# A transformer block on one Trainium2 core: branch projections in a written order, and the first group of gate reordered

## The chip, the core and the metric

The kernel is one program on one core of a Trainium2 chip. The core has five engines with instruction queues of their own: TensorE (PE) multiplies matrices, VectorE (DVE), ScalarE (ACT) and GpSimd (POOL) work on tiles elementwise, and SyncE (SP) issues the DMA transfers between the chip's memory (DRAM) and the on-chip buffer SBUF. Matrix products arrive in PSUM, eight banks of 128 x 512 floats. Each queue runs strictly in its own order; an instruction whose operand is not there holds up all behind it. The metric is the device time of one launch in microseconds (us), less is better.

## The reference

One layer of a diffusion backbone in fp32: 1024 latent tokens of width 1024 and 256 context tokens. After a modulated norm and one input projection come two branches, a neighbourhood attention (`o_na`) and a gated linear attention (`o_gla`). The part that matters here follows:

```python
y = sigmoid(m_a) * (o_na @ w_br_na) + sigmoid(m_b) * (o_gla @ w_br_gla)   # 512 -> 1024, twice
x = x + g1 * (y @ w_o)                                                    # 1024 -> 1024
h2 = modulate(rmsnorm(x, norm2_g), sh2, sc2)
x = x + g2 * ((silu(h2 @ w_gate) * (h2 @ w_up)) @ w_down)                 # 1024 -> 2816 -> 1024
```

## The kernel before

**Products in three passes.** Each fp32 operand is split into a high part (an ACT cast) and a low part (what is left, `raw - hi`, mostly on DVE, in places on POOL). A product is the sum of three matmul passes: high x high, high x low and low x high (`mm3`). So a weight page costs a DMA to one of three raw buffers (`load_raw`, 512 KB), a cast and a subtraction before PE can use it.

**Branch stage** (`branch_units`, before lines 1017 to 1048). For each branch b, half c of the output features, half hf of the tokens and block m, one tile of 128 features x 512 tokens: 12 matmuls into a bank of the pool `mm` (two banks, `psb`), then the merge: y = (1 + ta) * psb for the first branch, and for the second ta = (1 + ta) * psb and y = y + ta. `ta` is a gate tile that earlier code left in DRAM (`ma_d`, `mb_d`). That makes 32 tiles. The second weight half of a branch is split into the buffers of the first (`bufs=4`: two pages, high and low), so the splits can start only when the first half is used up. The output weights `w_out` are loaded after that, scaled by g1 on POOL (L1169), cast and subtracted, 8 pages. Nothing of this stage is written in an order across engines: a scheduler places the instructions by its own estimates of time.

**Output projection and norm** (`project`, `features2`): `pso` is y times the scaled output weights; its result goes to `h2`, the operand of the feed-forward part.

**First group of gate and up.** The feed-forward products use a Strassen-like scheme: for a group of 256 columns of `w_gate` or `w_up`, seven products P1 to P7 of 512-wide blocks take the place of eight. The right operands are B11, B21, B22 and the differences T1 to T4 of `h2`; the left operands are sums of weight blocks (`sums`, tiles `sc` on DVE), split into pages `w_P` (`put`). The results are added up through banks X, Y, Z and W:

```python
X = P1 + P2;  u2 = P1 + P6 (bank Y);  u3 = u2 + P7 (bank Z) + P5 (bank W)
u6 = u2 + P4 (bank Z again);  u2 = u2 + P3 (bank W again)
```

So P4 may write Z only after DVE has added P7's Z, and P3 may write W only after P5's W. P1 and P2 of groups 0 and 1 are made ahead. In this stretch PE, DVE and ACT are `in_order`: the program's order is their order. For group 0 the low parts of gate are on DVE and ACT in the written list (`parted`), those of up on POOL; the DVE list ends after gate's group 0, and the scheduler places later DVE work, the sums of group 1 among it, anywhere after the last operand split (`marks["split"]`).

**Down projection** (`multiply`): seven passes over 11 groups; the lower weight rows of each group are loaded to tiles of their own (`wr`).

## Time and profile before

| | us |
|---|---|
| median of 3 runs | 1617.56 (1615.93 to 1619.08) |
| the profiled execution | 1613.99 |
| its span, first to last instruction | 1612.2 |
| PE busy | 1534.8 (95%) |
| DVE busy | 1012.3 (63%) |
| ACT busy | 638.4 (40%) |
| POOL busy | 518.2 (32%) |

A trace row names the line, the engine, the operation and output<-inputs by the names in the program; L136 is the helper through which PE, DVE and ACT issue, so rows are told apart by tile names. `psd` is the input projection of the gates, `psb` the branch stage, `pso` the output projection, `fX` to `fW` gate and up, `psdn` the down projection. In brackets stands how long the engine was idle before the row and what ended it. Matmuls overlap: one takes 0.39 us, and the next starts 0.23 us later.

### The profile page before, as it was taken

The page shows a single profiled execution, that of the slowest core. Times are in us where ns is not written, and L with a number is a line of the kernel's source. Part 1 is how long each engine was busy: PE and PEld are TensorE (multiplying, and loading weights), DVE is VectorE, ACT ScalarE, POOL GpSimd, SP SyncE. Part 2 cuts the span into 40 slices and gives each one's busy share as a digit, 9 for nine tenths or more (in the row PEclk, how much of TensorE's full clock was granted, in tenths as well). Part 3 has the DMA queues.
Part 4 walks back from the last instruction along what each step waited for, and adds up shares of the span by engine and source line. Part 5 has one row for each costly group of instructions (what it writes and reads, how often), then busy time and mean ns, then how long its engine had stood idle before and what let it go on. Part 6 is the DMA issues. An engine that isn't in the chain of part 4 may idle for free. (4 is left out here: it accounts for less than half of the span.)

```text
span 1612.2 us, 21617 instructions
## 1 busy us (share of the span) xinstructions
PE 1534.8 (95%) x7884; PEld 1253.3 (78%) x7884; DVE 1012.3 (63%) x1593; ACT 638.4 (40%) x1221; POOL 518.2 (32%) x345
## 2 busy tenths in 40 slices
PE   6998999999989998999989997899999999999998
PEld 3777777888878786878868885788888888887886
DVE  4755567238877755453475677766666665778356
ACT  3433453148777752132122334233333323344442
POOL 3333000022111211210041423455555555255444
PEclk9999999999999999999999998999999999999999
DMA  9456576454333336516542333323333333774342
GB/s 332 129 174 209 183 244 216 137 155 126 108 113 104 96 101 202 164 60 215 190 163 80 117 121 113 124 97 109 106 120 108 98 98 118 249 273 150 96 147 98
DMA packets 171667, 235.49 MB, mean 146 GB/s; under 512 B 15580, under 2 KB 105628, under 8 KB 171560
## 3 DMA queue, kind: packets, MB, share of 16 engines
q1 hardware_dynamic: 171560, 234.11, 44.8%
q8 instruction: 62, 1.02, 0.3%
q14 instruction: 45, 0.37, 0.1%
HBM read 167.83 MB, written 66.24 MB: 145 GB/s over the span
## 5 line engine op out<-in xcount | busy, mean ns | idle before, releaser
L136 PE MATMUL psdn<-wd,a 128*128 128x512 f32 x924 | 211.7, 390 | 3.5 <-DVE a L136 1.5
L136 PEld LDWEIGHTS psdn<-wd,a 128*128 128x128 f32 x924 | 172.9, 188 | 42.2 <-DVE a L136 3.2
L210 POOL TENSOR_TENSOR w_P<-sc,w_P 128x512 fp32r<-128x512 f32 x84 | 122.4, 1459 | 131.0 <-ACT w_P L136 131.0
L136 PE MATMUL fZ<-T,w_P 128*128 128x512 f32 x528 | 129.9, 396 | 17.0 <-DVE u L136 17.0
L136 PE MATMUL psd<-hh,w_hi 128*128 128x512 f32 x320 | 132.8, 415 | 0.0
L136 PEld LDWEIGHTS fZ<-T,w_P 128*128 128x128 f32 x528 | 100.4, 191 | 39.9 <-issue 12.1
L210 POOL TENSOR_TENSOR w_lo<-raw,w_hi 128x1024 fp32r<-128x1024 f32 x24 | 57.7, 2408 | 219.0 <-ACT w_hi L136 206.9
L136 PE MATMUL psd<-hh,w_lo 128*128 128x512 f32 x320 | 127.5, 398 | 0.0
L136 PE MATMUL psj<-w_hi,hh 128*128 128x512 f32 x320 | 126.5, 397 | 0.6 <-ACT hh L136 0.6
L136 PE MATMUL psd<-hl,w_hi 128*128 128x512 f32 x320 | 126.6, 396 | 0.0
L136 PE MATMUL psj<-w_lo,hh 128*128 128x512 f32 x320 | 126.1, 394 | 0.3 <-POOL w_lo L210 0.3
L136 PE MATMUL psj<-w_hi,hl 128*128 128x512 f32 x320 | 125.7, 396 | 0.6 <-DVE r L136 0.3
L210 POOL TENSOR_TENSOR w_P<-raw,w_P 128x512 fp32r<-128x512 f32 x57 | 87.9, 1542 | 76.5 <-ACT w_P L136 75.2
L136 ACT CAST w_P<-sc 128x512 fp32r<-128x512 f32 x88 | 54.5, 621 | 139.1 <-PE fZ L136 80.6
L136 DVE TENSOR_TENSOR a<-ar,a 128x512 fp32r<-128x512 f32 x77 | 66.4, 870 | 59.6 <-ACT a L136 59.5
L136 PE MATMUL fX<-B,w_P 128*128 128x512 f32 x432 | 103.8, 389 | 0.0
L248 POOL TENSOR_TENSOR r<-r,nhalf 128x8 f32<-128x8 f32 (+1 forms) x40 | 50.6, 1268 | 150.3 <-DVE r L136 150.3
L136 PEld LDWEIGHTS fX<-B,w_P 128*128 128x128 f32 x432 | 81.1, 188 | 16.8
L136 ACT CAST a<-ar 128x512 fp32r<-128x512 f32 x77 | 47.9, 622 | 112.9 <-PE psdn L136 64.5
L136 ACT CAST w_hi<-raw 128x1024 fp32r<-128x1024 f32 x56 | 58.3, 1050 | 56.0 <-DMA raw<-in_w_in_dram 16.2
L210 POOL TENSOR_TENSOR wd<-wr,wd 128x512 fp32r<-128x512 f32 x39 | 59.3, 1526 | 50.7 <-ACT wd L136 50.4
L136 DVE SCALAR_TENSOR_TENSOR t1f<-t1f,u 128x512 f32<-128x512 f32 x66 | 59.6, 903 | 21.3 <-ACT t1f L136 20.3
(262 smaller groups left out, 3472.3 us busy)
## 6 DMA issues: line engine op xcount, KB each, us to landing
wm<-in_w_mod_dram SPq DMA_DIRECT2D x48, 512.0 KB
raw<-in_w_in_dram SPq DMA_DIRECT2D x40, 512.0 KB
ar<-s_d SPq DMA_DIRECT2D x77, 256.0 KB
raw<-in_w_gate_dram SPq DMA_DIRECT2D x22, 512.0 KB
raw<-in_w_up_dram SPq DMA_DIRECT2D x22, 512.0 KB
s_d<-t1f SPq DMA_DIRECT2D x44, 256.0 KB
s_d<-sa SPq DMA_DIRECT2D x33, 256.0 KB
xt<-in_x_dram SPq DMA_DIRECT2D x16, 512.0 KB
```

The source lines that it names most:

```text
L136: r = op(*args, **kw)
L210: return (lo_eng or DVE).tensor_tensor(lo, src, hi.bitcast(F32), op=ALU.subtract)
L248: POOL.tensor_tensor(r, r, nhalf[:, 0:w], op=ALU.pow)
```

## The change

SP becomes an engine whose order can be written. The generator for the branches gives way to `Pages`, an operand whose page has three separate steps, `load`, `high` and `low`, and to one loop over the 32 tiles in which PE, DVE, ACT and SP all keep the program's order. A table `steps` says at which tile each page is loaded; two tiles later it is cast, three tiles later its low part is made. The gate tile is fetched four tiles ahead (`LA`). From the place of the input stream, which is no longer needed, come eight buffers for weight halves instead of four, and room for the first half of the output weights (`tpa`), which are now prepared during the first 16 tiles; the second half follows from tile 17 on.

In the first group of gate the products come in the order P6, P7, P5, P4, P3 (before: P5, P7, P6, P4, P3); DVE's additions of Y and Z are written before the split of B22; the low parts of up's group 0 are made on DVE instead of POOL; and DVE's written list reaches to the end of gate's group 0, after which group 1's sums may begin. T1 and T3 move to `tpa`, and in the down projection the lower weight rows of groups 0 to 7 are loaded to their place.

```diff
-    PE, DVE, ACT = Ordered(nc.tensor), Ordered(nc.vector), Ordered(nc.scalar)
+    PE, DVE, ACT, SP = Ordered(nc.tensor), Ordered(nc.vector), Ordered(nc.scalar), Ordered(nc.sync)
...
-    def branch_units(pl, o_d, w_d, gate_d, first):
-        w = lambda c: load_w(pl, w_d[:, c * 512:(c + 1) * 512], 4, 512, tag="wb", bufs=4)
-        wc = w(0)
-        o = load_w(pl, o_d, 4, 1024, tag="o")
-        yield
-        for c in range(2):
-            for hf in range(2):
-                ts_ = slice(hf * 512, (hf + 1) * 512)
-                for m in range(4):
-                    f = 4 * c + m
-                    ta = page("ta", tag="sb")
-                    SP.dma_start(ta, gate_d[f * P:(f + 1) * P, ts_])
-                    ps = mm.tile([P, 512], F32, tag="mm", name="psb")
-                    mm3(ps, range(4), cut(wc, slice(m * P, (m + 1) * P)), cut(o, ts_))
-                    if first:
-                        DVE.scalar_tensor_tensor(y(hf, f), ta, 1.0, ps, op0=ALU.add, op1=ALU.mult)
-                    else:
-                        DVE.scalar_tensor_tensor(ta, ta, 1.0, ps, op0=ALU.add, op1=ALU.mult)
-                        DVE.tensor_tensor(y(hf, f), y(hf, f), ta, op=ALU.add)
-            if c == 0:
-                wc = w(1)
-        yield
...
-    with pool("d1", 8, side="right") as d1p:
-        bu = branch_units(d1p, ona_d, w_na, ma_d, True)
-        next(bu)
-        next(bu)
...
+    class Pages:
...
+        def load(self, i):
+            self.raws[i] = load_raw(self.src, i * self.per, self.per, self.n)
+
+        def high(self, i):
+            raw = self.raws[i]
+            if self.row is not None:
+                POOL.tensor_tensor(raw, raw, self.row.unsqueeze(1).broadcast_to([P, self.per, self.n]), op=ALU.mult)
...
+            ACT.copy(self.parts[i][0], raw)
+
+        def low(self, i):
+            hi, lo = self.parts[i]
+            DVE.tensor_tensor(lo, self.raws.pop(i), hi.bitcast(F32), op=ALU.subtract)
+
+        def operand(self):
+            return [(lambda k, u=u: self.parts[k // self.per][u][:, k % self.per]) for u in range(2)]
+
+    def out_weights(pl, c):
+        g1b = up0.tile([P, 512], F32, tag="u2", name="g1b")
+        SP.dma_start(g1b, mod_d[0:1, c * 512:(c + 1) * 512].broadcast_to([P, 512]))
+        whole = [block(pl, n).rearrange("p a k n -> p (a k) n") for n in ("wo_hi", "wo_lo")]
+        return Pages(pl, w_out[:, c * 512:(c + 1) * 512], None, None, g1b, whole)
...
+    def gate_tile(i):
+        if i < 32:
+            b, c, hf, m = i // 16, i // 8 % 2, i // 4 % 2, i % 4
+            f = 4 * c + m
+            tas[i] = page("ta", tag=("sb", "st")[i % 2])
+            SP.dma_start(tas[i], (ma_d, mb_d)[b][f * P:(f + 1) * P, halves[hf]])
+
+    def merge_tile(i, o, w, early):
+        b, c, hf, m = i // 16, i // 8 % 2, i // 4 % 2, i % 4
+        ps = mm.tile([P, 512], F32, tag="mm", name="psb")
+        mm3(ps, range(4), cut(w, slice(m * P, (m + 1) * P)), cut(o, halves[hf]))
+        early()
+        ta, yt_ = tas.pop(i), y(hf, 4 * c + m)
+        if b == 0:
+            DVE.scalar_tensor_tensor(yt_, ta, 1.0, ps, op0=ALU.add, op1=ALU.mult)
+        else:
+            DVE.scalar_tensor_tensor(ta, ta, 1.0, ps, op0=ALU.add, op1=ALU.mult)
+            DVE.tensor_tensor(yt_, yt_, ta, op=ALU.add)
...
+    d1p = s_d1.enter_context(pool("d1", 8, side="right"))
+    wn0 = Pages(d1p, w_na[:, halves[0]], "wb", 4)
+    on = Pages(d1p, ona_d, "o", 8)
+    for pg_, n in ((wn0, 2), (on, 4)):
+        for i in range(n):
+            for f in (pg_.load, pg_.high, pg_.low):
+                f(i)
     s1.close()
...
+    tpa = ctx.enter_context(pool("tpa"))
+    d2p = sb_.enter_context(pool("d2", 8))
+    wn1 = Pages(d2p, w_na[:, halves[1]], "wb", 8)
+    ogp = Pages(d2p, ogl_d, "o", 8)
+    wg0 = Pages(d2p, w_gla[:, halves[0]], "wb", 8)
+    wg1 = Pages(d2p, w_gla[:, halves[1]], "wb", 8)
+    wo0 = out_weights(tpa, 0)
+    steps = ([(wn1, i, t) for i, t in enumerate((0, 0))] + [(ogp, i, t) for i, t in enumerate((1, 2, 4, 5))]
...
+    for i in range(LA):
...
+    for e in (PE, DVE, ACT, SP):
+        e.in_order(True)
+    for t in range(32):
+        if t == 16:
+            s_d1.close()
+            tpl = sf.enter_context(pool("tpl", side="right"))
+            wo1 = out_weights(tpl, 1)
+        here = lambda d: [((p_ or wo1), i) for p_, i, t0 in steps if t0 + d == t]
...
+        for p_, i in here(0):
+            p_.load(i)
+        gate_tile(t + LA)
+        for p_, i in here(2):
+            p_.high(i)
+
+        def lows():
+            for p_, i in here(3):
+                p_.low(i)
+
+        merge_tile(t, (on, ogp)[t // 16].operand(), (wn0, wn1, wg0, wg1)[t // 8].operand(), lows)
+    for e in (PE, DVE, ACT, SP):
+        e.in_order(False)
+    wos = [wo0.operand(), wo1.operand()]
+    sb_.close()
...
-        wos = []
-        for c in range(2):
-            g1b = up0.tile([P, 512], F32, tag="u2", name="g1b")
-            SP.dma_start(g1b, mod_d[0:1, c * 512:(c + 1) * 512].broadcast_to([P, 512]))
-            w2 = [block(n).rearrange("p a k n -> p (a k) n") for n in ("wo_hi", "wo_lo")]
-            for k in range(0, KT, 2):
-                raw = load_raw(w_out[:, c * 512:(c + 1) * 512], k, 2, 512)
-                POOL.tensor_tensor(raw, raw, g1b.unsqueeze(1).broadcast_to([P, 2, 512]), op=ALU.mult)
-                hi_lo(w2[0][:, k:k + 2], w2[1][:, k:k + 2], raw)
...
-        tb["T1"], tb["T3"] = block("T1"), block("T3")
+        tb["T1"], tb["T3"] = block(tpa, "T1"), block(tpa, "T3")
...
         put0 = lambda *which: puts(pgs[0][1], sc, pgs[0][3][2], which, parted)
-        put0("P5", "P7")
+        put0("P6")
         spilled(0, 0)
...
-        put0("P6")
+        put0("P7", "P5")
         for q in range(4):
             if q == 2:
                 spilled(0, 1)
             split("T4", b21, q, (b21, b12))
         put0("P4", "P3")
+        low_parts()
         spilled(1, 1)
-        tb["B22"] = block("B22", "x", bufs=1)
-        for q in range(4):
-            split("B22", b22, q)
-        low_parts()
         pgs.append(lhs_pages(w_up, 0))
-        puts(pgs[1][1], pgs[1][2](), pgs[1][3][2], ("P5", "P7", "P6", "P4", "P3"))
         first = [(pg[0], X, u2) for pg, (_, X, u2) in zip(pgs, first)]
-        ACT.in_order(False)
 
...
+    ops0, X, u2 = first[0]
+    Y, Z, W = banks3()
+    u3 = page("u3")
+    product("P6", ops0, Y, True)
+    product("P7", ops0, Z, True)
+    product("P5", ops0, W, True)
+    DVE.tensor_tensor(u2, u2, Y, op=ALU.add)
+    DVE.tensor_tensor(u3, u2, Z, op=ALU.add)
+    tb["B22"] = block(tpl, "B22", "x", 1)
+    for q in range(4):
+        split("B22", b22, q)
+    low_parts()
+    first[0] += (Z, W, u3)
...
+    def first_gate(done):
+        ops_, X, u2, Z, W, u3 = first[0]
+        u6 = up.tile([P, 512], F32, tag="u6", name="u6")
+        product("P4", ops_, Z, False)
+        DVE.tensor_tensor(u3, u3, W, op=ALU.add)
+        product("P3", ops_, W, False)
+        pg = pgs[1]
+        puts(pg[1], pg[2](), pg[3][2], ("P6", "P7", "P5", "P4", "P3"), parted)
+        low_parts()
+        done(0, 0, X)
+        done(1, 1, u3)
+        DVE.tensor_tensor(u6, u2, Z, op=ALU.add)
+        done(1, 0, u6)
+        DVE.tensor_tensor(u2, u2, W, op=ALU.add)
+        done(0, 1, u2)
+        marks["split"] = DVE.last
+        DVE.in_order(False)
+        ACT.in_order(False)
...
-        if pre is not None:
-            product("P5", ops_, W, True)
-            product("P7", ops_, Z, True)
         product("P6", ops_, Y, True)
...
-        blocks_of(w_gate, g, gate_done, first[0] if g == 0 else None)
-        DVE.in_order(False)
+        if g == 0:
+            first_gate(gate_done)
+        else:
+            blocks_of(w_gate, g, gate_done)
...
+        def lower_rows(g):
+
+            if g >= 8:
+                return fp.tile([P, 2, 512], F32, name=f"wr{g}1")
+            if g % 4 == 0:
+                lower.append(tpa.tile([P, 4, 2, 512], F32, tag="t", name="lower", bufs=2))
+            return lower[-1][:, g % 4]
```

SP's queue in the branch stage, from the first load of output weights on, before (`raw` a weight page, `ta` a gate tile):

```order
L214 DMA raw_7968<-in_w_out_dram 128x2x512
L1028 DMA ta_7563<-ma_d_69 128x512
L1028 DMA ta_7579<-ma_d_69 128x512
L1028 DMA ta_7595<-ma_d_69 128x512
L1028 DMA ta_7653<-mb_d_70 128x512
L1028 DMA ta_7670<-mb_d_70 128x512
L1028 DMA ta_7687<-mb_d_70 128x512
L214 DMA raw_7973<-in_w_out_dram 128x2x512
L1028 DMA ta_7704<-mb_d_70 128x512
L1028 DMA ta_7721<-mb_d_70 128x512
L214 DMA raw_7978<-in_w_out_dram 128x2x512
L1028 DMA ta_7738<-mb_d_70 128x512
```

and now:

```order
L137 DMA raw_7530<-in_w_out_dram 128x2x512
L137 DMA ta_7532<-ma_d_69 128x512
L137 DMA raw_7552<-in_w_out_dram 128x2x512
L137 DMA ta_7554<-ma_d_69 128x512
L137 DMA ta_7574<-ma_d_69 128x512
L137 DMA raw_7593<-in_w_out_dram 128x2x512
L137 DMA ta_7595<-ma_d_69 128x512
L137 DMA raw_7614<-in_w_out_dram 128x2x512
L137 DMA ta_7616<-mb_d_70 128x512
L137 DMA ta_7633<-mb_d_70 128x512
L137 DMA raw_7651<-in_w_gla_dram 128x2x512
L137 DMA ta_7653<-mb_d_70 128x512
```

Before, one load of output weights stands ahead of the second branch's first gate tiles (`mb_d`) and the rest between these; now four do, and the loads stand singly between gate tiles.

VectorE's queue from the last operand part of gate's group 0 on, before (`sc` a sum of weight blocks, `raw_8961` of up's group 0, `raw_9167` of gate's group 1; `u2`, `u3` the sums over banks):

```order
L136 TENSOR_TENSOR w_P3_8945<-sc_8872,w_P3_8945 128x512
L136 TENSOR_TENSOR B22_8951<-h2_11_7951,B22_8951 128x4x128 x4
L136 TENSOR_TENSOR sc_8965<-raw_8961,raw_8963 128x512
L136 TENSOR_TENSOR sc_8966<-sc_8965,raw_8961 128x512
L136 TENSOR_TENSOR sc_8967<-raw_8961 128x512
L136 TENSOR_TENSOR sc_8968<-raw_8963,sc_8966 128x512
L136 TENSOR_TENSOR sc_9175<-raw_9167,raw_9169 128x512
L136 TENSOR_TENSOR sc_9177<-raw_9167 128x512
L136 TENSOR_TENSOR sc_9176<-sc_9175,raw_9167 128x512
L136 TENSOR_TENSOR sc_9178<-raw_9169,sc_9176 128x512
L136 TENSOR_TENSOR u2_8765<-u2_8765,fY_8997 128x512
L136 SCALAR_TENSOR_TENSOR t1f_9039<-t1f_9039,fX_8764 128x512
```

and now (`raw_8955` is of up's group 0):

```order
L137 TENSOR_TENSOR w_P3_8948<-sc_8875,w_P3_8948 128x512
L137 TENSOR_TENSOR u2_8768<-u2_8768,fY_8964 128x512
L137 TENSOR_TENSOR u3_8967<-u2_8768,fZ_8965 128x512
L137 TENSOR_TENSOR B22_9006<-h2_11_8005,B22_9006 128x4x128 x4
L137 TENSOR_TENSOR u3_8967<-u3_8967,fW_8966 128x512
L137 TENSOR_TENSOR sc_9045<-raw_8955,raw_8957 128x512
L137 TENSOR_TENSOR sc_9046<-sc_9045,raw_8955 128x512
L137 TENSOR_TENSOR sc_9047<-raw_8955 128x512
L137 TENSOR_TENSOR sc_9048<-raw_8957,sc_9046 128x512
L137 TENSOR_TENSOR w_P6_9053<-sc_9046,w_P6_9053 128x512
L137 TENSOR_TENSOR w_P7_9055<-sc_9047,w_P7_9055 128x512
L137 TENSOR_TENSOR w_P5_9058<-sc_9045,w_P5_9058 128x512
```

The additions of Y and Z stood behind eight sums; now they stand ahead of B22 and of up's sums, and the sums of group 1 come later.

TensorE's queue from the first of these products on, before (first five rows gate, then up):

```order
L136 MATMUL fW_8999<-T1_8742,w_P5_8877 128x512 x12
L136 MATMUL fZ_8998<-T3_8743,w_P7_8879 128x512 x12
L136 MATMUL fY_8997<-T2_8859,w_P6_8924 128x512 x12
L136 MATMUL fZ_8998<-T4_8860,w_P4_8942 128x512 x12
L136 MATMUL fW_8999<-B22_8951,w_P3_8945 128x512 x12
L136 MATMUL fW_9081<-T1_8742,w_P5_8973 128x512 x12
L136 MATMUL fZ_9080<-T3_8743,w_P7_8976 128x512 x12
L136 MATMUL fY_9079<-T2_8859,w_P6_8979 128x512 x12
```

and now:

```order
L137 MATMUL fY_8964<-T2_8862,w_P6_8880 128x512 x12
L137 MATMUL fZ_8965<-T3_8746,w_P7_8924 128x512 x12
L137 MATMUL fW_8966<-T1_8745,w_P5_8927 128x512 x12
L137 MATMUL fZ_8965<-T4_8863,w_P4_8945 128x512 x12
L137 MATMUL fW_8966<-B22_9006,w_P3_8948 128x512 x12
L137 MATMUL fY_9082<-T2_8862,w_P6_9053 128x512 x12
L137 MATMUL fZ_9083<-T3_8746,w_P7_9055 128x512 x12
L137 MATMUL fW_9084<-T1_8745,w_P5_9058 128x512 x12
```

P6 into Y moves to the front, P5 into W to the third place.

## Rows read from the trace of the kernel before

**Rows 1.** Page, first table: engine, busy us, share, instructions:

```profile
PE 1534.8 (95%) x7884; PEld 1253.3 (78%) x7884; DVE 1012.3 (63%) x1593; ACT 638.4 (40%) x1221; POOL 518.2 (32%) x345
```

**Rows 2.** Stretches, TensorE: us, busy, count, granted clock, DMA, GB/s:

```profile
758.61:857.93 99.32, 92.00 (x386) 0.97 0.49 164
974.37:1048.98 74.61, 58.14 (x241) 0.91 0.36 118
```

**Rows 3.** TensorE's time line, branch stage: start, duration, engine, line, operation:

```profile
758.61 0.39 PE L136 MATMUL psb<-w_hi 128*128 128x512 f32 x1
...
829.40 0.80 PE L136 MATMUL psb<-w_hi 128*128 128x512 f32 x1 [3.67 <-ACT w_hi L136]
...
842.42 0.50 PE L136 MATMUL psb<-w_hi 128*128 128x512 f32 x1 [2.87 <-DVE ta L136]
...
857.93 0.39 PE L136 MATMUL pso<-wo_hi,yh 128*128 128x512 f32 x1
```

**Rows 4.** Groups by form, branch stage: busy, mean ns, idle before:

```profile
L136 PE MATMUL psb<-w_hi 128*128 128x512 f32 x128 | 51.8, 405 | 7.0 <-ACT w_hi L136 3.7 <-DVE ta L136 3.3
...
L136 PE MATMUL psb<-w_hi,w_lo 128*128 128x512 f32 x128 | 50.9, 399 | 0.4 <-DVE w_lo L136 0.4
...
L1169 POOL TENSOR_TENSOR raw<-raw,g1b 128x1024 f32<-128x1024 f32 x8 | 20.8, 2600 | 96.9 <-DMA raw<-in_w_out_dram 89.8 <-issue 5.7 <-DVE ta L136 1.3
L136 DVE TENSOR_TENSOR y<-y,ta 128x512 f32<-128x512 f32 x15 | 16.4, 1096 | 0.3
L136 DVE TENSOR_TENSOR w_lo<-raw,w_hi 128x1024 fp32r<-128x1024 f32 x10 | 12.2, 1222 | 18.7 <-ACT w_hi L136 18.7
L136 DVE TENSOR_TENSOR wo_lo<-raw,wo_hi 128x1024 fp32r<-128x1024 f32 x8 | 11.0, 1376 | 7.5 <-ACT wo_hi L136 7.5
```

**Rows 5.** Time lines of GpSimd (first row) and VectorE near 835 us:

```profile
833.03 8.19 POOL L1169 TENSOR_TENSOR raw<-raw,g1b 128x1024 f32<-128x1024 f32 x3 [5.71 <-issue]
...
835.06 0.69 DVE L136 SCALAR_TENSOR_TENSOR ta<-ta,psb 128x512 f32<-128x512 f32 x1 [1.94 <-PE psb L136]
...
838.93 2.84 DVE L136 TENSOR_TENSOR y<-y,ta 128x512 f32<-128x512 f32 x1
```

**Rows 6.** Time lines, two loads: issue (SPq) and first user:

```profile
781.32 0.32 SPq L214 DMA_DIRECT2D raw<-ogl_d  x1
...
784.73 1.05 ACT L136 CAST w_hi<-raw 128x1024 fp32r<-128x1024 f32 x1 [1.57 <-DMA raw<-ogl_d]
...
788.07 0.39 SPq L214 DMA_DIRECT2D raw<-in_w_out_dram  x1
...
794.01 2.39 POOL L1169 TENSOR_TENSOR raw<-raw,g1b 128x1024 f32<-128x1024 f32 x1 [66.02 <-DMA raw<-in_w_out_dram]
```

**Rows 7.** Time line of TensorE, first groups of gate and up:

```profile
974.37 2.88 PE L136 MATMUL fW<-T,w_P 128*128 128x512 f32 x12
977.09 2.88 PE L136 MATMUL fZ<-T,w_P 128*128 128x512 f32 x12
...
994.42 5.46 PE L136 MATMUL fZ<-T,w_P 128*128 128x512 f32 x12 [11.72 <-DVE u L136]
...
1048.98 2.88 PE L136 MATMUL fX<-B,w_P 128*128 128x512 f32 x12
```

**Rows 8.** Waits, 980 to 1046 us: total us, times, longest:

```profile
PE fZ L136 <- DVE u L136: 16.5, 4, 11.7
```

**Rows 9.** Time line of VectorE, first groups of gate and up:

```profile
963.59 0.68 DVE L136 TENSOR_TENSOR sc<-raw 128x512 f32<-128x512 f32 x1
...
978.52 0.68 DVE L136 TENSOR_TENSOR w_P<-sc,w_P 128x512 fp32r<-128x512 f32 x1
...
981.77 0.68 DVE L136 TENSOR_TENSOR sc<-raw 128x512 f32<-128x512 f32 x1
...
987.46 2.56 DVE L136 TENSOR_TENSOR sc<-raw 128x512 f32<-128x512 f32 x2 [2.00 <-DMA raw<-in_w_gate_dram]
...
992.39 0.68 DVE L136 TENSOR_TENSOR u<-u,fY 128x512 f32<-128x512 f32 x1
```

More of the change, by code (lines that the diff above doesn't have):

```diff
@@ L64 @@
 NTAIL = 2
+LA = 4
 E1 = (1, 2)
@@ L120, in hybrid_block_kernel @@
     nc = tc.nc
-    POOL, SP = nc.gpsimd, nc.sync
+    POOL = nc.gpsimd
     sched = mybir.DependencyInfo(mybir.DependencyClass.NoSync, mybir.DependencyReason.SCHED_ONLY)
@@ new lines, in out_weights @@
+    def out_weights(pl, c):
[3 more added lines that the diff above has]
+        return Pages(pl, w_out[:, c * 512:(c + 1) * 512], None, None, g1b, whole)
+    halves = [slice(c * 512, (c + 1) * 512) for c in range(2)]
+    tas = {}
+    def gate_tile(i):
[4 more added lines that the diff above has]
+            SP.dma_start(tas[i], (ma_d, mb_d)[b][f * P:(f + 1) * P, halves[hf]])
@@ L1355, in blocks_of @@
                 X, u2 = first_block(ops_)
-        Y, Z, W = (fps.tile([P, 512], F32, tag=n, name="f" + n) for n in "YZW")
+        Y, Z, W = banks3()
         u3 = up.tile([P, 512], F32, tag="u3", name="u3")
         u6 = up.tile([P, 512], F32, tag="u6", name="u6")
-        if pre is not None:
-            product("P5", ops_, W, True)
-            product("P7", ops_, Z, True)
         product("P6", ops_, Y, True)
```

42 lines of the change are left out of this document (25 added, 17 removed).

## The prediction

> **What bounds the kernel now.** I read the page's first table, then the stretches of the whole program, then TensorE's own time line wherever a stretch is not full, and last, for each gap, the engine that ended it. TensorE (PE) is busy for 1534.8 us, 95% of the span [rows 1], and so the bound; it stands idle mainly in two places near the middle, where time can be won.
>
> The first place is the branch projections, 32 tiles of 12 matmuls (three groups of 128 [rows 4]). Undisturbed, 12 matmuls follow each other in 977.09 - 974.37 = 2.72 us [rows 7], so 32 tiles are worth 87.0 us. The first `psb` matmul starts at 758.61 and the first `pso` of the output projection at 857.93 [rows 3]: 99.3 us, so 12.3 are lost. TensorE idles for 7.4 of them: 7.0 before one group of `psb`, 0.4 before another [rows 3, 4]. The large gaps are 3.67 us, ended by an ACT cast of a weight page, and 2.87, ended by a DVE product [rows 3]. The other 4.9 is slow running after them: the first one takes 0.80 instead of 0.39 [rows 3] at a mean granted clock of 0.97 over the stretch [rows 2]. One microsecond of idling costs 12.3 / 7.4 = 1.66 here.
>
> The second place is the first group of gate and up. From P5 of gate at 974.37 to the first `fX` of group 2 at 1048.98 [rows 7] run 20 products (five each for gate and up of groups 0 and 1), worth 54.4 us; it takes 74.6, so 20.2 are lost at a granted clock of 0.91 [rows 2]. PE idles 16.5 us in four waits before `fZ`, all for DVE's `u`, the longest 11.7 [rows 8]; the product behind it takes 5.46 instead of 2.88 [rows 7]. DVE's rows say why: the last operand part of gate leaves at 978.52, but the sum u2 + Y that PE's P4 needs through Z starts only at 992.39, behind the sums of the up page and of group 1, whose raw page was still on its way (2.00 us of waiting at 987.46) [rows 9].
>
> **The change part by part.** No matmul is added or removed; the splits and sums are the same in number. What moves is order, and five low parts of up's first group go from GpSimd (POOL) to DVE. I therefore sum what of the 12.3 and the 20.2 us remains.
>
> *Branch stage, loads.* A page now has three steps: load at tile t, cast at t+2, low part at t+3. Half a megabyte issued at 781.32 is cast at 784.73, 3.4 us later; the slowest took 794.01 - 788.07 = 5.9 [rows 6]. Two tiles are 5.4 us, so a usual load is in time for its cast and a slow one 0.5 late, which the third step (2.72) covers, with the cast at 1.05 [rows 6]. The second weight halves, for which PE stood 3.67 us, are split by tile 4 (needed at tile 8) and by tile 18 (needed at 24): covered by six tiles. The gate tiles are issued four tiles ahead, 10.9 us. Without that cover each late page would cost what is late times 1.66.
>
> *Branch stage, SP's list.* All DMAs of the stage now sit in one written order, 18 raw pages and 28 gate tiles (four go ahead). A raw load waits for one of three buffers, and so do the gate tiles behind it. A buffer turns over in 3 tiles + 1.22 = 9.4 us, or, where the data are slow, in 5.9 + 2.6 + 1.05 + 1.22 = 10.8 [rows 4, 6]: 3.1 to 3.6 us a load, 56 to 65 us for 18, and the written steps span 24 tiles, 65 us. Cost 0.
>
> *Branch stage, DVE.* The densest part is tiles 17 to 25: nine merges of 0.69 + 0.69 and six low parts of 1.22, 19.7 us of DVE in 24.5 of PE [rows 4, 5]. POOL's four scalings of 2.60 fall in it. Where POOL runs, a DVE sum of two SBUF tiles stretches: 2.84 [rows 5] against 0.68 for such a sum elsewhere [rows 9], while the product that reads PSUM stays at 0.69 inside the same POOL stretch [rows 5]. Over the stage the 15 sums averaged 1.096 and the 8 output low parts 1.376 against 1.222 [rows 4]: 15 x 0.41 + 8 x 0.15 = 7.3 us for 8 scalings, 0.92 each. So 19.7 + 4 x 0.92 = 23.4 of 24.5. It is uneven: in tiles 20 to 22 and 23 to 25 each, 3 x 1.38 + 2 x 1.22 + 2 x 0.92 = 8.4 against 8.16, 0.25 late, twice. I take 0.5 for these and 0.4 at the first halves as now: 0.9 x 1.66 = 1.5 us remaining. The bounds are 0 (two banks of `psb` let a merge be late by some 2 us) and the full 2.60 for each scaling (first rival). Output weights of half 0 are now scaled and cast among the first 16 tiles, where a merge is 0.69 alone; that is what empties the second half. What the written order no longer allows, ACT making `yh` between the casts, is hidden in tiles 26 to 31, which have no low parts.
>
> *First group of gate.* PE now runs P6, P7, P5, P4, P3. DVE's list up to gate's last low part has the same 25 operations in another order, at 0.62 us each ((978.52 - 963.59) / 24 [rows 9]). T2 and w_P6 are out after 14 of them, at 972.3, before PE needs them at 974.37. After the 25th, at 979.1, come u2 + Y (979.7), u3 = u2 + Z (P7 ends 980.0; 980.7), four parts of B22 (983.2), u3 + W (P5 ends 982.7; 983.8). PE wants P4 at 974.37 + 3 x 2.72 = 982.5, when Z is free since 980.7, and P3 at 985.3, with W and B22 ready. Four sums and the first low part of up on DVE end at 986.9; PE wants up's P6 at 988.0. So the 11.7 us wait goes, and with it the slow product. What is late next is up's P6, with 1.1 us to spare, then P4 of the later products. The sums of group 1 now wait for the end of gate; they start near 994 and PE needs them at 1001.6. POOL, freed of five low parts, has these 7 us for the first of group 1. Of the three short waits (16.5 - 11.7 = 4.8 together) their order against DVE's `u` changes, and what remains is between 0 and 4.8; by the list all three are gone, by the old trace none, and I keep one, 1.4. Saved: 20.2 - 1.4 = 18.8 us.
>
> *Down projection.* The lower weight rows of eight groups now lie where T1 and T3 lay, free once PE has done P5 of the last up. Their first use follows a pass of 132 matmuls, 29.9 us at 2.72 for 12. Cost 0.
>
> **Sum.** 10.8 + 18.8 = 29.6 us. The profiled execution took 1613.99 us, so its like would take 1584.4; the median of the runs, 1617.56, lies 3.6 above it, so I forecast 1588.0.
>
> **Rivals.** *DVE is blocked in full by POOL (1596).* If each of the four scalings holds DVE for its whole 2.60, DVE needs 30.1 in 24.5 us: 5.6 late, 9.3 with the slow running, and the branch saves 3.0. Sum 21.8: 1595.8. For it stands the single sum of 2.84, against it the mean of 0.92. The Trainium skill, SBUF — State Buffer, section "Who interferes with whom", speaks for this rival: a DVE instruction with two SBUF inputs and a GpSimd one that reads SBUF exclude each other, and the loser waits for the whole instruction. The trace agrees on single rows [rows 5] and not on the mean, since a DVE sum often finds POOL idle.
>
> *The wait at gate moves on to up (1597).* If up's raw page or its low parts miss their 1.1 us by a landing, 3.5 us, and the three short waits stay, 8.3 us of idling at 20.2 / 16.5 = 1.22 cost 10.2. The group saves 10.0; with the branch 20.8: 1596.8. For it: DVE was full for 15 us before this point, and a raw page came late at 987.46. Against it: that was a page of group 1, and up's own sums began at 981.77 without a wait [rows 9].
>
> *Nothing moves (1617).* The scheduler's order could be carried out with the same waits, each gap filled from the next queue. Against it stands that nobody but DVE's list held back the 11.7 us.
>
> *SP's list chokes (1625), slower than before.* A raw load that waits for its buffer holds back gate tiles; a merge without its gate tile holds back the low part behind it on DVE, and so the buffer. Up to a turnover of 10.9 us (65 x 3 / 18) this costs nothing; it takes 16 to eat all gains. At 17 us 18 loads take 102 instead of 65: 1588 + 37 = 1625. Against it: the slowest landing seen gives 10.8.
>
> **How the numbers follow.** The forecast has 0.74, the first two rivals 0.10 each, no effect 0.03, the choking list 0.03. 0.2% of the time is 3.2 us, about what a measurement here tells from none. Faster is thus 0.94, same 0.03, slower 0.03. If all of both losses went it would be 1617.56 - 32.5 = 1585.1; runs spread by 3.2 us (1615.93 to 1619.08), so the range starts at 1582. Above, it takes in the first two rivals with the same spread: 1600.
>
> **What would show it.** Right: `psb` to `pso` in 87 to 90 us without a gap over 1 us and a granted clock of 1.00; gate's five products back to back behind `fE`; DVE's `u` on `fY` within 3 us of P6's end; the first `fX` of group 2 some 55 to 57 us after gate's first product. Wrong: a gap before `psb` ended by DVE's sum in tiles 20 to 25 (first rival); a gap before up's `fY` ended by `w_P` (second); raw loads on SP waiting over 3 us for a low part (the list); a new gap anywhere after 1050.

## The result, and the profile after

The changed kernel takes 1603.92 us (median of 4 runs, 1602.4 to 1607.23) against 1618.26 for the kernel before (4 runs), a ratio of 0.9916 with a 95% interval of 0.9903 to 0.9929. It is faster, as forecast, but by 14.3 us and not 29.6: 1603.9 lies above the range of 1582 to 1600. TensorE's share of the span is little changed, 96% (1535.6 us busy) against 95% [rows 1].

The place where the gain stayed is found by cutting the span where TensorE (PE) passes from one stage to the next. The next rows are such stretches, PE alone (columns as in [rows 2]), first of the kernel before, then of the changed one: the branch projections (of before in [rows 2]); the output projection; the first stretch of gate and up, here from `fE`'s first matmul to the first `fX` of group 2; the groups after it; the down projection.

```profile
857.93:963.49 105.56, 105.39 (x497) 1.00 0.35 110
963.49:1048.98 85.49, 69.02 (x289) 0.92 0.35 115
1048.98:1392.55 343.57, 343.01 (x1513) 1.00 0.36 116
1392.55:1612.20 219.65, 211.73 (x925) 1.00 0.49 161
```

```profile
759.42:849.78 90.36, 87.92 (x385) 1.00 0.54 181
849.78:955.36 105.58, 105.40 (x497) 1.00 0.35 110
955.36:1035.05 79.69, 68.85 (x290) 0.94 0.37 116
1035.05:1377.77 342.72, 342.72 (x1514) 1.00 0.37 118
1377.77:1600.60 222.83, 213.43 (x925) 0.99 0.49 158
```

Stage by stage the change is worth -9.0, 0.0, -5.8, -0.9 and +3.2 us; with 0.8 more ahead of the branch stage that is the 11.6 by which the spans differ. The branch stage gave nearly what was forecast (10.8). Gate and up gave 5.8 of 18.8, and the down projection, booked at nothing, took 3.2 back.

*Branch stage.* PE's time line has two waits of note left where [rows 3] had 3.67 and 2.87:

```profile
798.33 0.50 PE L137 MATMUL psb<-w_hi 128*128 128x512 f32 x1 [0.32 <-DVE y L137]
...
817.00 0.50 PE L137 MATMUL psb<-w_hi 128*128 128x512 f32 x1 [2.06 <-DVE ta L137]
```

The second stands at the start of tile 20 (counted from 0), among the last six low parts and four scalings of GpSimd (POOL). Ahead of it VectorE (DVE) lost 4.3 us in two operations that ran beside two of the scalings, a sum on y (0.69 alone) and a low part of a branch page (1.22 alone); the second of the scalings stands in a fence of its own:

```profile
810.26 2.75 DVE L137 TENSOR_TENSOR y<-y,ta 128x512 f32<-128x512 f32 x1
812.94 3.41 DVE L137 TENSOR_TENSOR w_lo<-raw,w_hi 128x1024 fp32r<-128x1024 f32 x1
```

```profile
812.78 2.49 POOL L1035 TENSOR_TENSOR raw<-raw,g1b 128x1024 f32<-128x1024 f32 x1 [0.31 <-DMA raw<-in_w_out_dram]
```

Over the stage the sums average 1025 ns, against 1096 in [rows 4]:

```profile
L137 DVE TENSOR_TENSOR y<-y,ta 128x512 f32<-128x512 f32 x15 | 15.4, 1025 | 0.5
```

The output low parts average 1756 ns (1376 before), but the slow ones (2.33 to 2.83) are the first three of the first half, around tiles 12 to 14, where they cost PE no more than the 0.32.

*First stretch.* The 11.7 us wait of [rows 8] is gone from gate, and from 973.16 on twelve products follow each other without a gap. But PE now waits twice elsewhere, and runs slowly behind each wait:

```profile
968.72 4.61 PE L137 MATMUL fY<-T,w_P 128*128 128x512 f32 x12 [2.30 <-ACT pc L137]
...
1014.52 4.37 PE L137 MATMUL fZ<-T,w_P 128*128 128x512 f32 x12 [8.54 <-DVE u L137]
```

A product is 2.88 when nothing is in its way [rows 7], so the two cost 2.30 + 1.73 and 8.54 + 1.49, together 14.1 us; from the end of `fE` (966.41) to 1035.05 are 68.6 us against 54.4 for 20 products, 14.2 lost. The slow running is the clock: 0.62 and 0.65 granted in the two products, between its levels of 1.2 and 2.4 GHz, and 1.00 between them.

```profile
968.72:973.16 4.44, 4.44 (x12) 0.62 0.19 64
...
1014.52:1018.73 4.21, 4.21 (x13) 0.65 0.58 195
```

What released the first product is read from ACT, whose list is an order written out by hand. `pc<-fE` copies a partial sum of the second group out of PSUM:

```profile
958.28 0.59 ACT L137 COPY pc<-fE 128x512 f32<-128x512 f32 x1 [0.76 <-PE fE L137]
...
962.68 0.59 ACT L137 COPY pc<-fE 128x512 f32<-128x512 f32 x1 [2.15 <-DMA c_d<-pc]
...
968.09 0.58 ACT L137 COPY pc<-fE 128x512 f32<-128x512 f32 x1
```

The third copy ends at 968.67 and `fY` begins at 968.72. `fY`, which is now the first tile that PE writes, lies in the bank that `fE` leaves; before, `fW` came first, from another bank. The copy itself is late since the second one had to wait 2.15 us for the page that the first was still being stored from.

The second wait is read from DVE. PE's P4 of gate in group 1 needs `fZ`, which the addition `u<-u,fZ` has to read first. P7, which fills it, began at 1000.38. The kernel before waited 1.39 us at this product (at 1028.15). Here is what DVE did until that addition came:

```profile
997.33 3.48 DVE L137 TENSOR_TENSOR sc<-raw 128x512 f32<-128x512 f32 x2
1000.73 1.78 DVE L137 TENSOR_TENSOR sc<-sc,raw 128x512 f32<-128x512 f32 x1
1002.43 0.67 DVE L137 TENSOR_TENSOR u<-u,fW 128x512 f32<-128x512 f32 x1
...
1003.63 1.78 DVE L137 SCALAR_TENSOR_TENSOR t1f<-t1f,u 128x512 f32<-128x512 f32 x1
1005.33 1.76 DVE L137 TENSOR_TENSOR sc<-raw,sc 128x512 f32<-128x512 f32 x1
1007.01 1.75 DVE L137 TENSOR_TENSOR sa<-t1f 128x512 f32<-128x512 f32 x1
1008.69 0.68 DVE L137 TENSOR_TENSOR u<-u,fY 128x512 f32<-128x512 f32 x1
1009.29 1.15 DVE L137 TENSOR_TENSOR t1f<-t1f 128x512 f32<-128x512 f32 x1
1010.36 1.75 DVE L137 TENSOR_TENSOR sc<-raw 128x512 f32<-128x512 f32 x1
1012.03 1.74 DVE L137 TENSOR_TENSOR sa<-t1f 128x512 f32<-128x512 f32 x1
1013.70 0.67 DVE L137 TENSOR_TENSOR u<-u,fZ 128x512 f32<-128x512 f32 x1
```

Two things are to be seen. DVE never rests, and what stands ahead of the addition are sums for blocks that come later (`sc` for up of group 1 and gate of group 2) and `sa` of group 0. And most of them take 1.75 us where they take 0.68 alone; in these 17 us POOL makes low parts of group 1, with one break of 1.4 us.

*Down projection.* Here are its first wait on PE (0.80 us in the kernel before), and ahead of it DVE and ACT, each in a fence of its own:

```profile
1409.99 2.50 PE L137 MATMUL psdn<-wd,a 128*128 128x512 f32 x5 [2.03 <-ACT u L137]
```

```profile
1403.45 0.69 DVE L137 TENSOR_TENSOR wr<-lower,wr 128x512 f32<-128x512 f32 x1 [3.93 <-DMA lower<-in_w_down_dram]
```

```profile
1404.17 0.62 ACT L137 CAST a<-ar 128x512 fp32r<-128x512 f32 x1 [4.33 <-DVE wr L137]
...
1409.37 2.04 ACT L137 COPY u<-psdn 128x512 f32<-128x512 f32 x4
```

DVE takes a difference for product 6 inside product 1's pass, waits for a lower row that has not landed, and ACT's cast waits for DVE; the copies that empty product 1's banks come late.

### The profile page after: what moved, and what is told of

It is laid out like the page before. It is cut to its first block, busy times and chain, and to the rows that moved or that the text cites. A ratio compares the mean times of both kernels' runs of the same rounds, so it can differ in the third digit from the quotient of the medians.

```text
span 1600.6 us, 21607 instructions
## 1 busy us (share of the span) xinstructions
PE 1535.6 (96%) x7884; PEld 1257.4 (79%) x7884; DVE 1017.5 (64%) x1598; ACT 637.8 (40%) x1221; POOL 516.4 (32%) x340
## 4 chain that ended last, share of the span: by engine, by line
PE 71%; DVE 12%; DMA 5%; issue 5%; ACT 4%; POOL 2%; SPq 1%; ACTq 0%; DVEq 0%; POOLq 0%
PE psdn L137 10%; PE psj L137 9%; PE psd L137 9%; PE fZ L137 7%; PE fW L137 7%; PE fX L137 6%; PE pso L137 5%; PE psb L137 4%; PE fY L137 4%; PE pv L137 2%; PE pt L137 1%; SPq L137 1%; ACT pb L137 1%; POOL r L249 1%; PE mp L137 1%
## 5 line engine op out<-in xcount | busy, mean ns | idle before, releaser
L137 ACT CAST w_hi<-raw 128x1024 fp32r<-128x1024 f32 x56 | 58.3, 1051 | 54.4 <-PE psj L137 15.3
L137 PEld LDWEIGHTS psj<-w_hi,hh 128*128 128x128 f32 x320 | 60.8, 190 | 14.7 <-ACT hh L137 2.0
```

What stands on the lines that cost most here:

```text
L137: r = op(*args, **kw)
```

## The experiments

Each ratio is to runs of the kernel before taken together with that run. The medians wandered by some 2 us from one set of runs to the next, single runs by more, and the start of the branch stage, which no edit touches, lay between 757.6 and 765.4 us in the profiles (758.6 in that of before). The verdicts therefore rest on the stages of each profile (us, from the starts of PE's rows) more than on the medians:

| run | branch | first stretch | groups | down | median | ratio to before, interval |
|---|---|---|---|---|---|---|
| before | 99.3 | 85.5 | 343.6 | 219.7 | 1618.26 | |
| changed | 90.4 | 79.7 | 342.7 | 222.8 | 1603.92 | 0.9916 (0.9903-0.9929) |
| e1 | 91.3 | 85.8 | 343.6 | 223.3 | 1610.50 | 0.9946 (0.9925-0.9968) |
| e2 | 99.2 | 78.0 | 342.7 | 221.5 | 1609.47 | 0.9933 (0.9910-0.9956) |
| e3 | 90.4 | 69.2 | 350.0 | 221.3 | 1600.60 | 0.9875 (0.9852-0.9898) |
| e4 | 88.7 | 77.2 | 342.7 | 222.7 | 1601.23 | 0.9883 (0.9858-0.9908) |
| e5 | 89.3 | 77.3 | 342.7 | 223.4 | 1601.52 | 0.9892 (0.9869-0.9916) |
| e7 | 88.9 | 69.3 | 346.1 | 221.6 | 1597.75 | 0.9869 (0.9840-0.9899) |
| e8 | 88.1 | 78.4 | 342.7 | 222.7 | 1600.86 | 0.9886 (0.9866-0.9905) |
| e9 | 90.3 | 79.4 | 343.6 | 220.8 | 1602.22 | 0.9895 (0.9873-0.9917) |
| e10 | 90.5 | 78.6 | 342.7 | 226.2 | 1605.70 | 0.9914 (0.9892-0.9936) |
| e11 | 90.3 | 68.8 | 351.2 | 220.9 | 1600.42 | 0.9890 (0.9864-0.9916) |
| e12 | 89.3 | 67.9 | 351.2 | 223.0 | 1600.73 | 0.9882 (0.9855-0.9908) |
| e13 | 89.6 | 68.2 | 345.3 | 222.0 | 1594.69 | 0.9854 (0.9834-0.9873) |
| e14 | 90.3 | 68.7 | 342.7 | 223.1 | 1592.13 | 0.9844 (0.9820-0.9868) |
| e15 | 90.5 | 79.3 | 342.7 | 219.5 | 1601.01 | 0.9889 (0.9869-0.9909) |
| e16 | 90.2 | 68.5 | 345.3 | 220.8 | 1591.65 | 0.9834 (0.9817-0.9852) |
| e17 | 89.4 | 68.4 | 342.7 | 220.2 | 1592.96 | 0.9826 (0.9806-0.9846) |

Without any wait the first stretch would be 65.3 us (10.9 for `fE`, [rows 7] behind its start at 963.49, and 20 products of 2.72) and the groups 342.7 (126 products).

**The two parts apart (e1, e2).** e1 is the changed kernel with the functions of the first group put back, e2 the kernel before with those of the changed one; their diffs are the parts of the change shown above.

> The changed kernel with the first group of gate and up put back as it was (P5, P7, P6 first, up's low parts ahead of gate's additions); the branch stage and the lower rows stay changed. Theory, that the two parts add up: the branch stage keeps its 90.4 us (99.3 before), the stretch from gate's first product to the first fX of group 2 is back at 73 to 76 us with one wait for a DVE addition near 11 us, and the down projection keeps its 2 us loss, so 1610 to 1613 us. Rival, that the branch change is what spoils the first group (pages, loads or POOL left in another state): that stretch is longer than 77 us and the time is 1614 or more.

> The kernel before with only the first group of gate and up as in the changed kernel; branch stage and lower rows as before. Theory, that the wait for DVE moves from gate's first group to group 1 whatever stands in front: fE's start to the first fX of group 2 goes from 85.5 to about 80 us, with a wait near 8 us in group 1, and the time is 1611 to 1614 us. Rival, that the first-group part is worth its 18.8 us by itself and the changed branch takes it away again: 68 us for that stretch, 1598 to 1602 us.

The parts are apart: e1 keeps the branch gain (91.3) and has the old 11.77 us wait back, e2 keeps the old branch and has 78.0 with a wait of 8.55 in group 1. So the branch change spoils nothing at gate; the wait in group 1 comes with the first-group part of the change by itself.

**Low parts to DVE (e3).**

```
-            puts(put, sums(...), a22, ("P6", "P7", "P5", "P4", "P3"))
+            puts(put, sums(...), a22, ("P6", "P7", "P5", "P4", "P3"),
+                 hi_lo if g == 1 else None)
```

> The changed kernel with the ten low parts of group 1's operands (gate and up) on DVE in place of POOL; nothing else is moved by hand. Theory, that DVE's additions come late since its operations take 1.75 us beside POOL's low parts and 0.68 us alone: with POOL silent there DVE's list is short enough though it is ten operations longer (10 x 0.62 = 6.2 us more, 12 x 1.1 = 13 us less), the 8.5 us wait in group 1 falls under 2 us and the slow product behind it goes, 1593 to 1597 us. Rival, that DVE simply has too many operations ahead of that addition: ten more make the wait 8 to 14 us, 1603 to 1609 us.

The wait in group 1 is gone, though DVE has ten operations more and the same five sums still stand ahead of the addition. Its list, at the place of the rows above, now runs at 0.69 each:

```profile
1006.61 0.69 DVE L137 TENSOR_TENSOR sc<-raw 128x512 f32<-128x512 f32 x1
...
1007.81 0.69 DVE L137 TENSOR_TENSOR u<-u,fZ 128x512 f32<-128x512 f32 x1
```

The rival, that there is too much in the list whatever it costs, falls for group 1. But the time missed its forecast of 1593 to 1597: the first stretch won 10.5 us and the groups lost 7.3, by the same kind of wait in group 2, where the low parts are POOL's again:

```profile
1047.59 2.93 PE L137 MATMUL fZ<-T,w_P 128*128 128x512 f32 x6 [4.46 <-DVE u L137]
```

**Another bank, another page (e4, e5).**

```
-        return (fps.tile([P, 512], F32, tag=n, name="f" + n) for n in "YZW")
+        b = {n: fps.tile([P, 512], F32, tag=n, name="f" + n) for n in "WZY"}
+        return b["Y"], b["Z"], b["W"]
```

```
-            pc = page("pc", tag=("st", "sb")[j])
+            pc = page("pc", tag=("st", "sb")[(i + j) % 2])
```

> The changed kernel with the PSUM tiles of the first products taken in the order W, Z, Y in place of Y, Z, W, so that gate's first product does not get the bank from which the second group's partial sum is copied out. Theory, that P6 waited for that bank alone (its copy ended at 968.67 and P6 began at 968.72): the 2.3 us wait goes, and with it the slow product behind it (4.4 in place of 2.9 us), 1599 to 1601 us. Rival, that PE gets to the wait in group 1 sooner and stands there longer, since DVE's list there does not follow PE: 1603 to 1605 us, with that wait at 11 to 13 us.

> The changed kernel with the page of the second copied-out partial sum taken from the other set of pages, so that it need not wait for the first one's store. Theory, that gate's first product was late by a chain on ACT (copy waits 2.15 us for a store, everything behind it in ACT's written order is late, the copy that frees the bank among it): the wait of ACT goes and PE's 2.3 us ahead of the first product falls under 0.5 us with the banks as they were; as in the run with other banks, the wait in group 1 stays near 9 us, so the stretch from fE to the first fX of group 2 is 77 us and the time 1600 to 1602 us. Rival, that the copy's place behind the second quarter of T4 in ACT's order is late enough by itself: the wait stays above 1.5 us and the time at 1603 to 1605 us.

In e4 the first product follows `fE` without a wait and takes 2.88, which shows the bank:

```profile
955.47 11.04 PE L137 MATMUL fE<-B,gx 128*128 128x512 f32 x48
966.35 2.88 PE L137 MATMUL fY<-T,w_P 128*128 128x512 f32 x12
...
1011.03 5.42 PE L137 MATMUL fZ<-T,w_P 128*128 128x512 f32 x12 [9.15 <-DVE u L137]
```

Against the changed kernel's profile the stretch won 2.5 us, not 4: the wait in group 1 grew from 8.54 to 9.15, and the product behind it took 5.42 in place of 4.37. This last is scatter, since it took 4.98 to 5.46 in e5, e8, e9 and e10 with the same wait. The five profiles that leave the stretch as it is (changed, e8, e9, e10, e15) took 78.4 to 79.7, so the bank is worth 1.3 to 2.5 us. In e5 the wait shrank to 0.87, not under 0.5; without either edit it was 1.53 to 2.39 in eight profiles, so the page makes about half of it. That the rest is the copy's place in ACT's list, behind casts that wait for DVE, is argued and not shown.

**The sums behind the addition (e7).** POOL keeps its low parts; only DVE's order changes.

```
-            puts(put, sums(after="split" if g == 1 else None), a22, (...))
+            puts(put, sums(after="split" if g == 1 and src is w_gate
+                           else "u3" if g <= 2 else None), a22, (...))
 ...
-        DVE.tensor_tensor(u3, u2, Z, op=ALU.add)
+        marks["u3"] = DVE.tensor_tensor(u3, u2, Z, op=ALU.add)
```

> The changed kernel with POOL's low parts where they were, but the sums of the blocks that follow (up of group 1, gate and up of group 2) put behind the addition of P7's bank of the block before them in DVE's list. Theory, that the 8.5 us wait needs both, the 1.75 us beside POOL and five sums ahead of the addition: without the sums it falls to 0 to 3 us though each operation still takes 1.75 us beside POOL, 1594 to 1598 us. Rival, that the contention alone makes it: the four other operations (sa, t1f) ahead of the addition still cost 7 us, the wait stays above 5 us, 1600 to 1604 us. A further way out: the sums are then too late for the next block's first operand, and a wait for POOL's w_P of 1 to 4 us stands there instead.

The wait at P4 of gate in group 1 is gone:

```profile
1002.12 3.01 PE L137 MATMUL fZ<-T,w_P 128*128 128x512 f32 x12
```

At P4 of up, five products later (1016.88), one of 0.51 appears. DVE's list shows why the first is gone: `u<-u,fZ` is done before the next block's sums begin. The operations just ahead of it are also short here: POOL stands idle from 997.58 to 1004.65, since the sums that its next low parts wait for come later.

```profile
999.37 0.68 DVE L137 TENSOR_TENSOR u<-u,fY 128x512 f32<-128x512 f32 x1
...
1001.29 0.68 DVE L137 TENSOR_TENSOR u<-u,fZ 128x512 f32<-128x512 f32 x1
1001.89 1.29 DVE L137 TENSOR_TENSOR sc<-raw 128x512 f32<-128x512 f32 x2
```

So either edit removes the wait. e3 keeps the order and takes POOL's work away, and so shows that the order alone does not make it. e7 does not part the two, since the new order takes POOL's work away from this place as well: how long the wait would be with the sums behind the addition and POOL at work is not shown. Some came back later: in group 2 a wait of 1.41 for an ACT copy, and two near 0.6 for DVE additions, the groups 3.4 us longer.

**Without POOL's scalings of the second half (e8).**

```
-            if self.row is not None:
+            if self.row is not None and self.pl is tpa:
                 POOL.tensor_tensor(raw, raw, ...)
```

> The changed kernel without POOL's scaling of the second half of the output weights by the gate row (those four multiplications are left out). Theory, that the 2 us gap in the branch stage comes from DVE's merge sums and these four scalings holding each other: the gap near tile 21 goes, DVE's sums there take 0.69 us in place of 2.2 to 2.8, and the stage takes 87.5 to 88.5 us in place of 90.4; the whole 1601 to 1604 us. Rival, that DVE is late there by its own count (two merge operations and a low part of 1.3 us a tile against 2.72 us): the gap stays above 1 us.

This version leaves a factor out of half of the output weights, so that only its time counts. The wait in tile 20 is gone, the stage takes 88.1, and the sums on y average 692 ns (1025 above):

```profile
L137 DVE TENSOR_TENSOR y<-y,ta 128x512 f32<-128x512 f32 x15 | 10.4, 692 | 0.5
```

The size of the wait is also a matter of chance: with the scalings in place a wait for `ta` in tiles 20 to 23 was 1.64 to 2.24 in nine profiles (the changed kernel's among them), 0.48 to 0.65 in e5, e7, e12, e13 and e17, and 0.22 in e4, though none of these edits touches the stage. Only e8 has none. Its stage is the shortest of all, by no more than 0.6 us (e4 took 88.7); what bears out the scalings as the cause is the sums at 692 ns together with the wait that every other profile has.

**Lower rows ahead (e9), and the changed kernel again (e10).** e9 loads the first four lower rows before the stage's loop (`ahead = {g: w_rows(lower_rows(g), g, 1) for g in range(4)}`).

> The changed kernel with the first four lower rows of the down weights loaded ahead of the down projection's own loop. Theory, that the 2.0 us wait behind product 1 of the down projection came from a lower row that SP issued at 1399.97 behind loads of spilled activations and landed at 1403.4, where DVE and behind it ACT stood: the wait falls under 1 us, the down projection takes 220 to 221.5 us in place of 222.8, the whole 1601 to 1603 us. Rival, that these waits are an effect of which list DVE gets and come back elsewhere: 222 to 224 us, no change.

> The changed kernel once more, without an edit, beside the versions below on the same chip. Every theory: 1602 to 1605 us, the 8.5 us wait in group 1 and the 2.0 us one in the down projection at their places.

The wait behind product 1 falls to 0.26 and the stage to 220.8, but a wait of 1.42 us for a DVE addition appears 3.6 us into the stage, and in e12 the same edit gave nothing (a wait of 2.53): the question was left to e15. In e10 the waits stand at their places, the one in group 1 at 8.55, that of the down projection at 3.44 in place of 2.03: 226.2 us for the stage.

**Two edits (e11, e12).** Banks as in e4, order as in e7 without up of group 2; e12 has e9's edit too.

> The changed kernel with two edits: the PSUM tiles in the order W, Z, Y, and the sums of the next block behind the addition of P7's bank for up of group 1 and gate of group 2 alone (up of group 2 is left to itself). Theory, that the two waits are apart from each other: the stretch from fE's start to the first fX of group 2 takes 65.5 to 68 us (79.7 in the changed kernel; 65.3 without a wait), the groups behind it 342.7 to 344 in place of 346.1, and the time is 12 us under the changed kernel, 1590 to 1593 us. Rival, that they share one delay (PE waits at the next place for what it no longer waits for here): 70 us or more for that stretch and 1595 or more.

> The same with the first four lower rows loaded ahead as well. Theory, that the loss in the down projection adds up with the others: 2 us less in that stage (220.8 in place of 222.8), 1588 to 1591 us. Rival, that the loads ahead take the place of others at the end of the groups (a 1.4 us wait for a DVE addition behind them): no difference to the run with two edits.

The first stretch came near its forecast of 65.5 to 68 (68.8, 67.9), the whole did not: 5.81 us of waiting turned up in group 2, in the block whose successor had been left to itself.

```profile
1047.09 1.22 PE L137 MATMUL fZ<-T,w_P 128*128 128x512 f32 x2 [5.81 <-DVE u L137]
```

**Order in group 2, in all groups, and the rows back (e13 to e17).** e13 is e11 with `g <= 2` for both blocks, e14 the same with `g <= 10`. e15 is the changed kernel with

```
-            if g >= 8:
+            if g < NG - 1:
                 return fp.tile([P, 2, 512], F32, name=f"wr{g}1")
```

> The changed kernel with the PSUM tiles in the order W, Z, Y and the sums behind the addition of P7's bank for up of group 1 and both blocks of group 2 (the run before left up of group 2 to itself, and a 5.8 us wait for a DVE addition stood there). Theory, that DVE owes work from the first groups and that the order of its list alone decides whether PE has to wait for it: the 5.8 us wait goes, first stretch 66 to 69 us, groups behind it 344 to 347 us, 1589 to 1595 us. Rival, that DVE beside POOL has too little time for a group: the wait moves on to group 3 at 3 us or more, and the time stays at 1598 to 1601 us.

> The same with the sums behind that addition in all groups. Theory: as the run with two groups, 343 to 347 us for the groups, no wait over 2 us, 1588 to 1595 us. Rival, that in the later groups the sums then come too late for POOL's low parts: waits of 0.5 to 2 us for w_P in every group, 1600 us or more.

> The changed kernel with ten of the eleven lower rows of the down weights in pages of the pool that opens with the stage, as in the kernel before (the last stays in T1's place). Theory, that the down projection loses its 1 to 3 us since a lower row in T1's or T3's place is loaded in another order, and DVE and ACT stand for it ahead of product 1's copies: the wait there falls from 2 to 3.4 us to under 1, the stage takes 219.5 to 221 us in place of 222.8 and 226.2, the whole 1601 to 1602.5 us. Rival, that the stage's time wanders with the loads whatever the rows' place: 221 to 224 us.

> All three edits: banks W, Z, Y, the sums behind the addition in groups 1 and 2, and ten lower rows as before. Theory, that the losses add up: 1587 to 1592 us, the fastest of all. Rival: no better than the run with banks and order alone.

> The changed kernel with the PSUM tiles in the order W, Z, Y, the sums behind the addition of P7's bank in all groups, and ten lower rows as before. Theory, that the three losses are apart: first stretch 68 to 69 us, groups 342.7, down projection 219.5 to 221, so 1586 to 1591 us and a ratio to the kernel before near 0.982. Rival: a stage takes back what another gains, 1592 us or more.

e13 and e14 settle it: with the sums behind the addition the wait does not move on to group 3. In e14 the groups take 342.7 us, 126 products without a gap; what is left in the first stretch is 1.11 and 0.51:

```profile
1007.97 3.00 PE L137 MATMUL fZ<-T,w_P 128*128 128x512 f32 x12 [1.11 <-DVE u L137]
...
1022.74 3.00 PE L137 MATMUL fZ<-T,w_P 128*128 128x512 f32 x12 [0.51 <-DVE u L137]
```

In e15 the down projection's first wait falls to 0.18 and the stage to 219.5:

```profile
1413.73 1.45 PE L137 MATMUL psdn<-wd,a 128*128 128x512 f32 x5 [0.18 <-ACT u L137]
```

DVE waits for a lower row here as well, but is released 21.6 us into the stage, in place of 25.7 in the changed kernel:

```profile
1405.10 0.69 DVE L137 TENSOR_TENSOR t<-wr,wr 128x512 f32<-128x512 f32 x1 [3.39 <-DMA wr<-in_w_down_dram]
```

Over all profiles the stage took 219.5 to 221.5 with the rows as before (before, e2, e15 to e17) and 220.9 to 226.2 in the changed way (eleven runs, without e9 and e12): medians of 220.2 and 222.7. The wait behind product 1 parts the two cleanly, with 0.80 at most in the five and 1.73 to 3.44 in the eleven. So the rows' place costs about 2.5 us; why their loads come later with it is not shown.

e17 has banks, order in all groups and rows as before, and its stages came out as expected:

```profile
765.44:854.82 89.38, 88.11 (x385) 1.00 0.55 183
854.82:960.39 105.57, 105.40 (x497) 1.00 0.35 110
960.39:1028.80 68.41, 66.51 (x289) 1.00 0.43 135
1028.80:1371.52 342.72, 342.72 (x1513) 1.00 0.37 118
1371.52:1591.70 220.18, 212.19 (x925) 1.00 0.49 161
```

Its median of 1592.96 lies 2 us over the expected 1586 to 1591, with a branch stage that began at 765.4, the latest of all. By the medians e17 cannot be told from e14 (1592.13), which has the rows in the changed way, nor from e16 (1591.65, within its expected 1587 to 1592), which has the order in groups 1 and 2 alone: their intervals overlap. At 0.9826 (0.9806 to 0.9846) it beats the kernel before and, with intervals that do not touch, the changed one.

## Why the prediction missed

- *The bound and the two places* were right: PE at 95%, and the gaps were to be won in the branch stage and at gate.
- *Branch stage* ("1.5 us remaining", 10.8 saved): right in mechanism and nearly in size. 3.3 of 90.4 us remain over 87.0, and 8.0 to 10.6 were saved in the runs that have this part as it is (e8 and e2 apart). Loads and SP's list cost PE no wait, as reckoned, though the sign set for the list did show: four raw loads on SP waited 3.9 to 7.0 us for a low part. The term that came out too small is 0.92 us for each scaling, a mean over all eight scalings of the kernel before, where only four operations of DVE were held up (sums of 2.48, 2.84 and 2.85 us and a low part of 2.47). In the changed kernel's second half four are held up by four scalings (sums of 2.75, 2.15 and 2.17 us, a low part of 3.41), 7.2 us or 1.8 each; by the prediction's own sum DVE needs 19.7 + 7.2 = 26.9 us in 24.5, and the wait was 2.06. The first rival's sign, a wait ended by DVE in tiles 20 to 25, did appear, with 1.8 a scaling in place of the rival's 2.60 and 3.3 us lost in place of 9.3. The low part of 3.41 ran from 812.94 beside a scaling that ended at 815.27. The Trainium skill, SBUF — State Buffer, "Who interferes with whom", says that the loser waits for the whole instruction; this row agrees.
- *First group, the wait at gate*: the wait of 11.7 us at P4 went, DVE's `u<-u,fY` came at 973.37, right behind P6, up's P6 had no wait. Every step of DVE's list up to there held.
- *First group, the start* ("T2 and w_P6 are out ... before PE needs them at 974.37"): the operands were in time, but the prediction asked only for operands. The first product also needs a bank, and by the new order it was the one that `fE` had just filled (e4). That is 4.0 us in the changed kernel's profile, of which e4 won 1.3 to 2.5. The sign "gate's five products back to back behind `fE`" failed here.
- *First group, what is late next* ("up's P6, with 1.1 us to spare, then P4 of the later products"; of the three short waits "I keep one, 1.4"): this is the step that failed. P4 of a later product it was, at 8.54 + 1.49 us. Group 1's operations were not listed and priced one by one; it got 7 us of room, with the remark that POOL "has these 7 us", and 1.4 us for what is left of three waits. But POOL at work is what takes DVE from 0.68 to 1.75, a price that the prediction had read in the branch stage [rows 5] and did not carry over; e3 shows it. And DVE's list behind gate was not read: five sums of later blocks stand ahead of the addition that frees the bank; e7, and in group 2 e13 against e11, show that moving such sums takes the wait away. With the old wait at gate gone the wait came one group later (e2), and with group 1 mended another group later (e3, e11). That DVE had used the old wait to catch up is a reading of this; no run tests it by itself, and e14 shows that with another order DVE has time enough.
- *The second rival* ("the wait at gate moves on to up") had the right thought and the wrong place and cause: the wait moved past up of group 0, for an addition and not for a page.
- *Down projection* ("Cost 0"): wrong by about 2.5 us (e15). The lower rows are not first used a pass later: DVE takes their differences for product 6 within the first pass. The sign "a new gap anywhere after 1050" appeared here (2.03 us at 1409.99).
- *Sum*: 29.6 less 1.8 (branch), 13.0 (first stretch) and 3.2 (down) is 11.6, the difference of the two spans (the groups' 0.9 and the 0.8 ahead of the branch cancel). Between the medians the gain is 14.3, since the profiled run of before lay 4.3 us under its median and that of the changed kernel 1.5 under its own.

## What to carry to other kernels

When a long wait is taken out, ask what the engine that ended it does next: here the wait came back at the next place where that engine's list had later work ahead of what frees a buffer. Read that list to the end of the next two blocks, put the operation that frees a bank ahead of work for later blocks, and price every two-input DVE operation by whether POOL is at work beside it. Of the first product in a new order ask not only whether its operands are there but also whose bank it writes.
